# First stage of a hybrid RWKV-7 and neighbourhood-attention layer: another order of loads, modulation pieces and token tiles

## The chip, the cores and the metric

The kernel runs on one core of a Trainium2 chip. The metric is the device time of one execution in microseconds; of several runs the median is taken.

## The reference

One layer of a diffusion backbone works on 512 latent tokens and 128 context tokens of width 1024. Only its beginning matters here:

```python
def _modulation(cvec, w_ada, b_ada):
    m = jax.nn.silu(cvec) @ w_ada + b_ada
    return jnp.split(m[..., None, :], 6, axis=-1)

def _trunk_layer(x, cvec, s0, ctx_k, ctx_v, p):
    sh1, sc1, g1, sh2, sc2, g2 = _modulation(cvec, p["w_ada"], p["b_ada"])
    h = _rmsnorm(x, p["norm1_g"]) * (1.0 + sc1) + sh1
    u_rw, u_na, gate_rw, gate_na = jnp.split(h @ p["w_in"], IN_SPLITS, axis=-1)
    ...
```

A conditioning vector (one for the latent tokens, one for the context tokens) gives a shift and a scale for every channel. The tokens are normalised, scaled and shifted to `h`, and `h` is multiplied by the input weights. Everything else of the layer (the two branches, their merging, the feed-forward part) follows and is the same in both kernels.

## The kernel before

The 640 tokens are five tiles of 128: tiles 0 to 3 are latent, tile 4 is the prompt. The 1024 channels are eight chunks of 128. The first stage has these parts, all in one loop body written out by hand:

- `x_load(i)` loads token tile i (512 KB). `norm_x(i)` normalises it (ScalarE squares, GpSimd takes the power, VectorE scales into `xn`), transposes it on TensorE in eight pieces (`xt`, line 408) and copies it to `xT`, four chunks by VectorE and four by ScalarE.
- `ada_part(k0, n, c0)` is a generator that loads the modulation's weights (`wa`, line 392) for the n chunks from k0 on, and multiplies them with the conditioning vectors on TensorE (`psa`, line 261, a narrow matmul with 32 columns of weights). Each call of `next` issues one load of 512 KB and the matmuls of the load before: one step.
- `mod_part(k0, n, c0)` copies the result out of PSUM (`rows`), transposes it (`pc`, line 419), forms the factors `A` and `B`, and then computes `h` for its chunks: ScalarE the high part (line 432), VectorE the exact value `ht` (line 434) and the low part (line 436). High and low parts let each product be formed from three single matmuls. It does tokens 0 to 511 first, and after a `yield` the prompt.
- `wload` loads a 512 KB piece of projection weights (`wst`, two buffers), casts it to a high part `whi` on ScalarE (line 192) and a low part `wlo` on VectorE (line 195); each has two buffers. A piece serves two chunks.
- `tok_gen` is the projection of one block of 512 output columns: 5 token tiles x 8 chunks x 3 products = 120 matmuls of 128x512 into five accumulators (`acc`, line 311). The first block's generator is `qg`; three such blocks (q, k, v) follow one another, 360 matmuls in all.

The modulation comes in three pieces: chunks 0 and 1, chunks 2 and 3, and chunks 4 to 7. The table `qp` says how many matmuls of `qg` stand between one modulation step and the next:

```python
    qp=((0, 0, 7, 6, 7), (2, 5, 4, 4, 3, 2, 5, 3, 1)), ada=2, pa=1, pd=0,
```

Within this stage TensorE runs in the order in which the code is written. The other engines and the queue of the SyncE engine (SP), which issues almost all loads, get their order from a scheduler at build time. It puts loads that later stages need into the queue where it sees room: the tables of relative positions (`win`, line 858), small projection weights (`upw`, `gup`, line 615 and after), and weights for the second modulation (`f` and `wa`, line 1025).

Of the kernel before, what the change touches and what calls it, by code (L numbers as in the profile page):

```python
# [15 lines left out]
NT = 640  # L16
# [98 lines left out]
def body(ctx: ExitStack, tc: tile.TileContext, xs, xp, cols, consts, w_ada, b_row, w_rw, w_qkv,  # L115
# [88 lines left out]
    def wload(src, eng=None):  # L204
        return wcast(wdma(src), eng)
# [78 lines left out]
            pass  # L284
        return pss

    def tok_gen(pss, pp, lhs_hl, chunks, kts, toks, tag="acc", bufs=5, tail=1, keep=None, eng=None, late=()):


        pss.update((i, pp.tile([P, 512], F32, tag="tp" if i == 5 else tag, bufs=3 if i == 5 else bufs,  # L290
                               name=nm("acc"))) for i in toks)
        lhs = lhs_hl if callable(lhs_hl) else lambda p_, kt, ts_: lhs_hl[p_][:, kt, ts_]
        last = len(kts) - 1
        ws, n0 = [] if keep is None else keep, len(chunks) - tail
        for ci, src in enumerate(chunks):
            ws.append(src if isinstance(src, (tuple, list)) else wload(src, eng))
            ks = [2 * ci + k for k in range(2)]

            if ci >= n0:
                order = [(ki, i) for i in toks for ki in range(2 * n0, last + 1)] if ci == len(chunks) - 1 else ()  # L300
            else:
                order = [(ki, i) for tk in (toks[:4], toks[4:]) for ki in ks for i in tk]
            ns = ((0, 1), (2,)) if ci in late else ((0, 1, 2),)
            for n, ki, i in ((n, *p_) for g in ns for p_ in order for n in g):
                kt = kts[ki]
                hi, lo = ws[ki // 2]
                ts_ = slice(min(i, 4) * 128, min(i, 4) * 128 + 128)
                a, b = (256 * (i - 4), 256 * (i - 3)) if i > 3 and 5 in toks else (0, 512)
                cs_ = slice(ki % 2 * 512 + a, ki % 2 * 512 + b)
                for x, w in (((0, hi), (1, hi), (0, lo))[n],):  # L310
                    pe.matmul(pss[i][:, a:b], lhs(x, kt, ts_), w[:, cs_], start=ki == 0 and n == 0,  # L311
                              stop=ki == last and n == 2)
                    yield
# [42 lines left out]
    hh, hl = hilo("h")  # L356
# [23 lines left out]
    xt, q0 = [], []  # L380

    def x_load(i):
        x = sb.tile([P, 1024], F32, tag="x", bufs=XB, name=nm("x"))
        sp.dma_start(x, xs[i * 128:(i + 1) * 128, :] if i < 4 else xp)
        xt.append(x)

    def wa_load(k0, n, kt):

        w = sb.tile([P, 1024], F32, tag="wa", bufs=WAB, name=nm("wa"))
        for i in range(4 // n):  # L390
            wv = w_ada[(kt + i) * 128:(kt + i + 1) * 128, 0:2048].rearrange("p (g c) -> p g c", g=2)
            sp.dma_start(V(w[:, :], [[128 * n, 2], [1, 128 * n]], i * 256 * n), wv[:, :, 128 * k0:128 * (k0 + n)])
        return w

    def ada_part(k0, n, c0):
# [7 lines left out]
    def norm_x(i):  # L403
        xn = tok_norm(sb, xt[i])
        for q in range(2):
            ps = pp.tile([P, 512], F32, tag="tp", name=nm("xt"))
            for k in range(4):
                pe.transpose(ps[:, k * 128:(k + 1) * 128], xn[:, (4 * q + k) * 128:(4 * q + k + 1) * 128], ident)
            (act.copy if q else dve.tensor_copy)(xT[:, 4 * q:4 * q + 4, i * 128:(i + 1) * 128],
                                                 V(ps[:, :], [[128, 4], [1, 128]]))  # L410

    def mod_part(k0, n, c0):

        m_ = n // 2
        rows = sb.tile([P, 256], F32, tag="rows", bufs=1, name=nm("rows"))
        dve.tensor_copy(rows[:, :64 * n], psa[:, c0:c0 + 64 * n])
        pc = pp.tile([P, 512], F32, tag="tp", name=nm("pc"))
        for q in range(m_):
            pe.transpose(pc[:, q * 128:(q + 1) * 128], rows[:, q * 128:(q + 1) * 128], ident)
        for j, m in ((2, A), (3, A), (0, B), (1, B)):  # L420
            kt = k0 + m_ * (j % 2)
            dve.tensor_tensor(out=m[:, kt:kt + m_, :], in0=V(pc[:, :], [[128, m_], [1, 2]], 32 * j),
                              in1=V(C[:, :], [[1, m_], [0, 2]], CO["bada"] + 8 * (j // 2) + kt), op=ALU.add)
        ks = slice(k0, k0 + n)
        dve.scalar_tensor_tensor(out=A[:, ks, :], in0=A[:, ks, :], scalar=1.0,
                                 in1=V(C[:, :], [[1, n], [0, 2]], CO["n1"] + k0), op0=ALU.add, op1=ALU.mult)
        for g, (a, b) in enumerate(((0, 512), (512, NT))):
            if g:
                yield
            for kt in range(k0, k0 + n):  # L430
                t = sb.tile([P, 512], F32, tag="ht", bufs=2, name=nm("ht"))[:, :b - a]
                act.activation(hh[:, kt, a:b], xT[:, kt, a:b], AF.Identity, bias=B[:, kt, g:g + 1],
                               scale=A[:, kt, g:g + 1])
                dve.tensor_scalar(out=t, in0=xT[:, kt, a:b], scalar1=A[:, kt, g:g + 1],
                                  scalar2=B[:, kt, g:g + 1], op0=ALU.mult, op1=ALU.add)
                dve.tensor_tensor(out=hl[:, kt, a:b], in0=t, in1=hh[:, kt, a:b].bitcast(F32), op=ALU.subtract)  # L436
# [5 lines left out]
    with s0:  # L442
        with tc.manual_schedule(engines=START):
            g = ada_part(0, 2, 0)
            for i in range(4):
                x_load(i)
                next(g, None)
                if i:
                    norm_x(i - 1)
            for _ in g:  # L450
                pass
            norm_x(3)
            q0.append(wload(w_qkv[0]))
            x_load(4)
            mod = mod_part(0, 2, 0)
            next(mod)
            psq = {}
            qg = tok_gen(psq, pp, (hh, hl), q0 + [w_qkv[i] for i in range(1, 4)], list(range(8)), range(5))
# [7 lines left out]
            g = ada_part(2, 2, 128)  # L466
            for i, n in enumerate(PRM["qp"][0]):
                next(g, None)
                some_q(n)
                if i == 2:  # L470
                    norm_x(4)
                    drain(mod)
            drain(mod_part(2, 2, 128))
            g = ada_part(4, 4, 256)
            for n in PRM["qp"][1]:
                next(g, None)
                some_q(n)
            drain(mod_part(4, 4, 256))
# [133 lines left out]

    def prep_dma(ct, S, upw, eng=sp):
        S.upw = upw
        eng.dma_start(upw[:, 0:512], lup[ct, :, 0:512])
        S.gup = kp.tile([P, 128], F32, tag="gup", bufs=2, name=nm("gup"))
        eng.dma_start(S.gup, lup[ct, :, 512:640])

    def prep_cast(S):
        upw = S.upw  # L620
# [219 lines left out]
    with s1:  # L840
# [13 lines left out]
        def window(ft, n):  # L854

            hd, ty = divmod(n, 3)
            win = p1.tile([P, 249], F32, tag="win", bufs=2, name=nm("win"))
            sp.dma_start(win[:, :249], bass.AP(rpbp.tensor, rpbp.offset + (2 * ft + hd) * 465 + 8 * ty,
                                               [[1, 16], [31, 8], [1, 249]]))
            bm = bms[(ft % 2) * 6 + n]  # L860
            pool.tensor_tensor(
                out=V(bm[0][:, :], [[bm[2], 2], [8, 16], [1, 8]], bm[1]),
                in0=V(win[:, :], [[-16, 2], [-1, 16], [-31, 8]], 248),
                in1=V(nam[:, :], [[16, 2], [1, 16], [0, 8]], 32 * ty), op=ALU.add)
# [69 lines left out]
        with ExitStack() as s1b:  # L934
# [86 lines left out]
            def ada_w(g, kt):  # L1021
                ws = [tb.tile([P, 1024], F32, tag="wa", bufs=2, name=nm("wa")), f5()[:, 0:1024]]
                for i, w in enumerate(ws):
                    c = g * 2048 + i * 1024
                    sp.dma_start(w, w_ada[kt * 128:(kt + 1) * 128, c:c + 1024])
                return ws

            def ada_gen():
# [1151 lines left out]
```

## Time and profile before

| | |
|---|---|
| three runs | 1141.27, 1141.41, 1143.85 us; median 1141.41 us |
| profiled execution, from its first to its last instruction | 1142.3 us |
| TensorE busy with matmuls | 97% of the span |
| VectorE, ScalarE, GpSimd busy | 68%, 47%, 17% |
| first stage, up to the first matmul of the second projection block | 62.6 us |

The profile is one execution of its own. It lists no time beside its span, which lies between the shortest and the longest of the runs. In its rows PE is the matmul part of TensorE and PEld its loading of weights, DVE is VectorE, ACT is ScalarE, POOL is GpSimd and SP is the queue of loads. L311 is line 311 of the kernel. A row of the time line has a start, a length in us, the engine, and what was done; in square brackets stands how long the engine was idle before, and what ended that. PEclk is the clock that TensorE was granted, 1.00 being full speed. A busy matmul's length includes its way through the array, so that matmuls overlap in the rows; their pace is read from their starts.

### The profile page before, as it was taken

To read this page: it belongs to the slowest core of one execution; us is meant where nothing else is said; L and a number is where in the kernel's file an instruction comes from. 1 tells how busy PE (TensorE), PEld (TensorE's weight loads), DVE (VectorE), ACT (ScalarE), POOL (GpSimd) and SP (SyncE) were. 2 spreads that over 40 slices of the span, in tenths; PEclk is the share of its full clock that TensorE was granted. 3 is DMA by queue.
4 is the path that set the end of the run, shared out by engine and by line. 5 is a ranking of instruction groups with operands and counts; after the bars stand their busy time and mean duration, and the time that the engine had idled before them with its cause. 6 is when DMAs were issued, how large, how long until landed. Compare 5 with 4: busy or idle time off the path is not lost.

```text
span 1142.3 us, 26868 instructions
## 1 busy us (share of the span) xinstructions
PE 1108.0 (97%) x11160; PEld 980.2 (86%) x11160; DVE 777.2 (68%) x1641; ACT 537.9 (47%) x1060; POOL 195.8 (17%) x262
## 2 busy tenths in 40 slices
PE   5999999999999999999899999999999999999998
PEld 4688878789888988888898788999899989998997
DVE  4565465669658847945787846996478647874775
ACT  4444566665565665567343525654134413441340
POOL 1163244330101212110100511210101010101000
PEclk8999999999999999999999999999999999999999
DMA  9753677654423433344734962223212321232122
GB/s 340 262 107 102 187 268 259 200 151 112 126 64 98 130 104 94 107 108 107 266 92 126 264 214 72 78 89 112 72 56 93 111 74 56 93 106 80 56 93 93
DMA packets 60482, 149.16 MB, mean 131 GB/s; under 512 B 7460, under 2 KB 22436, under 8 KB 60360
## 3 DMA queue, kind: packets, MB, share of 16 engines
q1 hardware_dynamic: 54312, 129.85, 34.8%
q0 software_dynamic: 4032, 14.68, 6.5%
q10 hardware_dynamic: 2016, 2.90, 0.8%
q8 instruction: 88, 1.44, 0.5%
q14 instruction: 34, 0.28, 0.1%
HBM read 118.41 MB, written 14.32 MB: 116 GB/s over the span
## 4 chain that ended last, share of the span: by engine, by line
PE 76%; DVE 8%; issue 7%; ACT 4%; DMA 3%; POOL 1%; SPq 0%; ACTq 0%; DVEq 0%; POOLq 0%
PE acc L311 23%; PE f L1883 23%; PE fl L223 10%; PE mm L223 5%; DMA wa<-in_w_ada_dram 3%; PE psa L1044 1%; DVE RL L1330 1%; DVE pr L1326 1%; PE lg L959 1%; PE pt L988 1%; PE po L1006 1%; DMA win<-in_rpbp_dram 1%; PE w L1446 1%; PE fl L587 1%; PE w L1189 1%
## 5 line engine op out<-in xcount | busy, mean ns | idle before, releaser
L1883 PE MATMUL f<-t,whi 128*128 128x320 f32 x640 | 141.7, 310 | 0.2
L311 PE MATMUL acc<-whi,u 128*128 128x512 f32 (+1 forms) x448 | 136.1, 386 | 0.0
L1883 PE MATMUL f<-b,whi 128*128 128x320 f32 x608 | 135.0, 310 | 0.4 <-DVE b L212 0.4
L223 PE MATMUL fl<-h,whi 128*128 128x320 f32 x672 | 120.9, 320 | 0.0
L1883 PEld LDWEIGHTS f<-t,whi 128*128 128x128 f32 x640 | 106.8, 188 | 0.8 <-issue 0.4
L223 PEld LDWEIGHTS fl<-h,whi 128*128 128x128 f32 x672 | 101.2, 188 | 4.8 <-issue 0.2
L192 ACT CAST whi<-wst 128x1024 fp32r<-128x1024 f32 (+1 forms) x77 | 79.3, 1033 | 53.4 <-PE acc L311 41.6
L1883 PEld LDWEIGHTS f<-b,whi 128*128 128x128 f32 x608 | 101.8, 188 | 1.1 <-issue 0.6
L1883 PE MATMUL f<-t,wlo 128*128 128x320 f32 x320 | 98.9, 309 | 0.0
L311 PEld LDWEIGHTS acc<-whi,u 128*128 128x128 f32 x448 | 83.5, 188 | 16.6
L1883 PE MATMUL f<-b,wlo 128*128 128x320 f32 x304 | 94.1, 309 | 0.0
L1936 ACT CAST whi<-ws 128x1024 fp32r<-128x1024 f32 x40 | 42.0, 1051 | 104.4 <-PE f L1883 45.6
L1950 POOL TENSOR_TENSOR ws<-wst 128x512 f32<-128x512 f32 x20 | 29.2, 1462 | 334.6 <-DVE wlo L1939 226.3
L311 PE MATMUL acc<-wlo,u 128*128 128x512 f32 (+1 forms) x224 | 86.3, 385 | 0.0
L311 PE MATMUL acc<-whi,h 128*128 128x512 f32 x240 | 79.2, 404 | 0.8 <-DVE h L436 0.8
L195 DVE TENSOR_TENSOR wlo<-wst,whi 128x1024 fp32r<-128x1024 f32 (+2 forms) x57 | 60.2, 1066 | 27.8 <-ACT whi L192 27.2
L1751 DVE SCALAR_TENSOR_TENSOR tt<-acc,G 128x512 f32<-128x512 f32 (+1 forms) x51 | 34.7, 680 | 59.6 <-PE acc L311 44.7
L223 PE MATMUL fl<-h,wlo 128*128 128x320 f32 x336 | 62.7, 318 | 0.0
L1936 ACT CAST whi<-wst 128x1024 fp32r<-128x1024 f32 (+1 forms) x48 | 41.3, 869 | 42.3 <-PE acc L311 37.6
L1883 PEld LDWEIGHTS f<-t,wlo 128*128 128x128 f32 x320 | 60.1, 188 | 0.0
L1939 DVE TENSOR_TENSOR wlo<-ws,whi 128x1024 fp32r<-128x1024 f32 x40 | 55.5, 1387 | 5.4 <-ACT whi L1936 5.4
L191 POOL DMA_DIRECT2D wlo<-wst x28 | 24.8, 886 | 191.4 <-ACT wlo L190 169.9
(341 smaller groups left out, 2534.0 us busy)
## 6 DMA issues: line engine op xcount, KB each, us to landing
wst<-in_w_dram SPq DMA_DIRECT2D x66, 512.0 KB
wst<-in_w_rw_dram SPq DMA_DIRECT2D x31, 512.0 KB
wlo<-wst POOLq DMA_DIRECT2D x28, 512.0 KB, 4.7
wa<-in_w_ada_dram SPq DMA_DIRECT2D x24, 512.0 KB
f<-in_w_ada_dram SPq DMA_DIRECT2D x16, 512.0 KB
wst<-in_w_qkv_dram SPq DMA_DIRECT2D x12, 512.0 KB
o<-o_d SPq DMA_DIRECT2D x14, 320.0 KB
x<-in_xs_dram SPq DMA_DIRECT2D x8, 512.0 KB
```

The lines of the kernel that those rows point to most:

```text
L191: pool.dma_start(lo[:, :n].bitcast(F32), st[:, :n], accum_op=ALU.add)
L192: act.copy(hi[:, :n], st[:, :n])
L195: dve.tensor_tensor(out=lo[:, a:b], in0=st[:, a:b], in1=hi[:, a:b].bitcast(F32), op=ALU.subtract)
L223: pe.matmul(ps[:, :t1 - t0], w[:, a:a + 128], x[:, k0 + kt, t0:t1], start=n == 0, stop=n == 3 * nk - 1)
L311: pe.matmul(pss[i][:, a:b], lhs(x, kt, ts_), w[:, cs_], start=ki == 0 and n == 0, stop=ki == last and n == 2)
L587: pe.matmul(ps[hf][:, :H2], u[:, kt * 128:kt * 128 + 128], x[:, kt, a:b], start=kt == 0 and n == 0, stop=kt == 7 and n == 2)
L959: pe.matmul(psl[:, hd, o_:o_ + n], qT[ft][rows, qs], x[rows, :], start=True, stop=True)
L1751: dve.scalar_tensor_tensor(out=tt, in0=ps[:, a:b], scalar=c, in1=G[:, g, sl], op0=ALU.mult, op1=ALU.mult)
L1883: pe.matmul(ps[:, :H2], w_[:, c_], x_[:, kt, :], start=first and kt + n == 0, stop=last and kt == 3 and n == 2, skip_group_check=more)
L1936: act.copy(r[0][:, :width], src())
L1939: dve.tensor_tensor(out=r[1][:, :width], in0=src(), in1=r[0][:, :width].bitcast(F32), op=ALU.subtract)
L1950: eng_x(PRM["se"][i - 1]).tensor_tensor(out=o_, in0=x, in1=y, op=op)
```

## The change

Four edits go together in the first stage.

1. Loads of later stages (`win`, the second modulation's weights, and the first `upw` and `gup`) are pinned behind the last modulation weights that the code has issued for this stage, by an ordering without a wait on an engine (`pin`).
2. The modulation comes in four pieces of two chunks each. The loads for chunks 4 to 7 are sixteen transfers of 256 KB where eight of 512 KB were. The first piece computes `h` in three groups of tokens: 0 to 255, 256 to 511, and the prompt.
3. The prompt's tile is loaded later, and its matmuls on the first two pieces of projection weights come behind those of the other four tiles (`steps`).
4. `qp` is now three rows of small commands: a number is so many matmuls, `a` a modulation step, `w` the load of the second piece of projection weights, `x` and `n` load and normalise the prompt's tile, `m` finishes a piece of modulation and modulates the latent tokens, `t` modulates the prompt's for the pieces done so far.

```diff
-    qp=((0, 0, 7, 6, 7), (2, 5, 4, 4, 3, 2, 5, 3, 1)), ada=2, pa=1, pd=0,
+    qp=("a a w 7 a x 3 a 2 m 12", "a 6 a 6 n a t 6 a 3 m 9", "t 6 a a 6 a 6 a 3 m t"), ada=2, pa=1, pd=0,
...
-            ws.append(src if isinstance(src, (tuple, list)) else wload(src, eng))
+            ws.append(src if isinstance(src, (tuple, list)) else src() if callable(src) else wload(src, eng))
...
+            if steps and ci < len(steps):
+                order = steps[ci]
...
+    urgent = []
+
+    def pin(ins):
+        tc.add_manual_dep(ins.ins, urgent[-1].ins.name, mybir.DependencyInfo(
+            mybir.DependencyClass.NoSync, mybir.DependencyReason.DATA), reason="order")
...
-    def mod_part(k0, n, c0):
+    def mod_part(k0, n, c0, groups):
...
-        for g, (a, b) in enumerate(((0, 512), (512, NT))):
-            if g:
-                yield
+        for (a, b) in groups:
+            yield
+            g = int(a >= 512)
...
-            norm_x(3)
             q0.append(wload(w_qkv[0]))
-            x_load(4)
-            mod = mod_part(0, 2, 0)
+            g = ada_part(2, 2, 128)
+            next(g)
+            mod = mod_part(0, 2, 0, ((0, 256), (256, 512), (512, NT)))
+            next(mod)
+            norm_x(3)
+            next(mod)
             next(mod)
...
+            steps = ([(k, i) for k in (0, 1) for i in four],
+                     [(2, i) for i in four] + [(0, 4), (1, 4)] + [(3, i) for i in four] + [(2, 4), (3, 4)])
+            chunks = q0 + [lambda: wcast(q0[1])] + [w_qkv[i] for i in (2, 3)]
...
+                    elif e == "m":
+                        drain(g)
+                        mod = mod_part(k0, 2, 64 * k0, ((0, 512), (512, NT)))
+                        next(mod)
+                        next(mod)
+                        todo.append(mod)
+                        if k0 < 6:
+                            g = ada_part(k0 + 2, 2, 64 * k0 + 128)
```

How the instructions stand now is shown at three places. The first is the SP queue behind the first piece's modulation weights (`wst` projection weights, `x` from `in_xp_dram` the prompt's tile). Before:

```order
L174 DMA wst_251<-in_w_qkv_dram 128x1024
L384 DMA x_257<-in_xp_dram 128x1024
L392 DMA wa_284<-in_w_ada_dram 128x2x256 x2
L392 DMA wa_295<-in_w_ada_dram 128x2x256 x2
L392 DMA wa_306<-in_w_ada_dram 128x2x256 x2
L392 DMA wa_356<-in_w_ada_dram 128x2x256 x2
L392 DMA wa_405<-in_w_ada_dram 128x2x512
```

and from there, some rows on:

```order
L858 DMA win_1024<-in_rpbp_dram 128x1x249
L858 DMA win_1027<-in_rpbp_dram 128x1x249
L392 DMA wa_440<-in_w_ada_dram 128x2x512
L615 DMA upw_1217<-in_lup_dram 128x512
L1025 DMA f_221_1297<-in_w_ada_dram 128x1024
L1025 DMA f_260_1486<-in_w_ada_dram 128x1024
L174 DMA wst_543<-in_w_qkv_dram 128x1024
L392 DMA wa_450<-in_w_ada_dram 128x2x512
```

Now:

```order
L174 DMA wst_232<-in_w_qkv_dram 128x1024
L400 DMA wa_238<-in_w_ada_dram 128x2x256 x2
L400 DMA wa_301<-in_w_ada_dram 128x2x256 x2
L400 DMA wa_312<-in_w_ada_dram 128x2x256 x2
L174 DMA wst_315<-in_w_qkv_dram 128x1024
L400 DMA wa_337<-in_w_ada_dram 128x2x256 x2
L386 DMA x_340<-in_xp_dram 128x1024
L400 DMA wa_384<-in_w_ada_dram 128x2x256 x2
```

```order
L400 DMA wa_579<-in_w_ada_dram 128x2x256 x2
L174 DMA wst_635<-in_w_qkv_dram 128x1024
L887 DMA win_1080<-in_rpbp_dram 128x1x249
L887 DMA win_1083<-in_rpbp_dram 128x1x249
L644 DMA upw_1273<-in_lup_dram 128x512
```

The prompt's tile moved behind four `wa` rows of two transfers each and a piece of projection weights, and `win`, `upw` and `f` behind the last `wa`.

The second place is TensorE at the start of the projection (`h_89` and `h_93` are the high and low parts of chunks 0 and 1). Before:

```order
L408 MATMUL xt_239<-K,xn_233 128x128 x4
L408 MATMUL xt_245<-K,xn_233 128x128 x4
L419 MATMUL pc_261<-K,rows_259 128x128
L261 MATMUL psa<-wa_284,cs 32x128 x8
L261 MATMUL psa<-wa_295,cs 32x128 x8
L311 MATMUL acc_309<-whi_253,h_89 128x512
L311 MATMUL acc_309<-whi_253,h_93 128x512
```

Now:

```order
L428 MATMUL pc_243<-K,rows_241 128x128
L417 MATMUL xt_257<-K,xn_251 128x128 x4
L417 MATMUL xt_263<-K,xn_251 128x128 x4
L261 MATMUL psa<-wa_238,cs 32x128 x8
L261 MATMUL psa<-wa_301,cs 32x128 x8
L313 MATMUL acc_317<-whi_234,h_89 128x512
L313 MATMUL acc_317<-whi_234,h_93 128x512
```

`pc` moved ahead of the transposes of token tile 3.

The third place is the prompt's tile and the third modulation piece, which stands only in the change: on TensorE

```order
L417 MATMUL xt_421<-K,xn_415 128x128 x4
L417 MATMUL xt_427<-K,xn_415 128x128 x4
L261 MATMUL psa<-wa_405,cs 32x128 x8
L313 MATMUL acc_321<-whi_234,h_89 128x512
L313 MATMUL acc_321<-whi_234,h_93 128x512
```

and, six matmuls and a step later,

```order
L313 MATMUL acc_317<-wlo_388,h_90 128x512
L261 MATMUL psa<-wa_474,cs 32x128 x8
L428 MATMUL pc_490<-K,rows_488 128x128
L313 MATMUL acc_318<-whi_387,h_90 128x512
L313 MATMUL acc_318<-whi_387,h_94 128x512
```

and on VectorE

```order
L445 TENSOR_TENSOR h_94<-ht_456,h_90 128x128
L195 TENSOR_TENSOR wlo_545<-wst_542,whi_544 128x1024
L425 COPY rows_488<-psa 128x128
L431 TENSOR_TENSOR A<-pc_490,C 128x2 x2
L431 TENSOR_TENSOR B<-pc_490,C 128x2 x2
```

The accumulator of the prompt's tile (`acc_321`) starts right behind one modulation step, `pc_490` follows its last step with no matmul between, and the `rows` that it reads stands behind a `wlo` on VectorE.

More of the change, by code (lines that the diff above doesn't have):

```diff
@@ L285, in tok_block, with tok_gen @@
         return pss
-    def tok_gen(pss, pp, lhs_hl, chunks, kts, toks, tag="acc", bufs=5, tail=1, keep=None, eng=None, late=()):
+    def tok_gen(pss, pp, lhs_hl, chunks, kts, toks, tag="acc", bufs=5, tail=1, keep=None, eng=None, late=(), steps=None):
         pss.update((i, pp.tile([P, 512], F32, tag="tp" if i == 5 else tag, bufs=3 if i == 5 else bufs,
@@ L391, in wa_load @@
             wv = w_ada[(kt + i) * 128:(kt + i + 1) * 128, 0:2048].rearrange("p (g c) -> p g c", g=2)
[L392 removed]
+            urgent.append(sp.dma_start(V(w[:, :], [[128 * n, 2], [1, 128 * n]], i * 256 * n),
+                                       wv[:, :, 128 * k0:128 * (k0 + n)]))
         return w
@@ L451, in body @@
                 pass
+            q0.append(wload(w_qkv[0]))
+            g = ada_part(2, 2, 128)
+            next(g)
+            mod = mod_part(0, 2, 0, ((0, 256), (256, 512), (512, NT)))
+            next(mod)
             norm_x(3)
-            q0.append(wload(w_qkv[0]))
-            x_load(4)
-            mod = mod_part(0, 2, 0)
+            next(mod)
             next(mod)
             psq = {}
-            qg = tok_gen(psq, pp, (hh, hl), q0 + [w_qkv[i] for i in range(1, 4)], list(range(8)), range(5))
+            four = list(range(4))
+            steps = ([(k, i) for k in (0, 1) for i in four],
+                     [(2, i) for i in four] + [(0, 4), (1, 4)] + [(3, i) for i in four] + [(2, 4), (3, 4)])
+            chunks = q0 + [lambda: wcast(q0[1])] + [w_qkv[i] for i in (2, 3)]
+            qg = tok_gen(psq, pp, (hh, hl), chunks, list(range(8)), range(5), steps=steps)
             derived()
@@ L464, in some_q @@
                     next(qg)
[L466 to L478, printed above, removed]
+            todo = [mod]
+            for k0, row in zip((2, 4, 6), PRM["qp"]):
+                for e in row.split():
+                    if e.isdigit():
+                        some_q(int(e))
+                    elif e == "a":
+                        next(g, None)
+                    elif e == "w":
+                        q0.append(wdma(w_qkv[1]))
+                    elif e == "x":
+                        x_load(4)
+                    elif e == "n":
+                        norm_x(4)
+                    elif e == "t":
+                        while todo:
+                            drain(todo.pop(0))
+                    elif e == "m":
[6 more added lines that the diff above has]
+                            g = ada_part(k0 + 2, 2, 64 * k0 + 128)
             tc.keep_in_program_order(act.dma_start(K[:, 128:], consts[:, 128:KO["nam"]]))
@@ L614, in prep_dma @@
         S.upw = upw
-        eng.dma_start(upw[:, 0:512], lup[ct, :, 0:512])
         S.gup = kp.tile([P, 128], F32, tag="gup", bufs=2, name=nm("gup"))
-        eng.dma_start(S.gup, lup[ct, :, 512:640])
+        for dst, a, b in ((upw[:, 0:512], 0, 512), (S.gup, 512, 640)):
+            ins = eng.dma_start(dst, lup[ct, :, a:b])
+            if not ct:
+                pin(ins)
     def prep_cast(S):
@@ L857, in window @@
             win = p1.tile([P, 249], F32, tag="win", bufs=2, name=nm("win"))
-            sp.dma_start(win[:, :249], bass.AP(rpbp.tensor, rpbp.offset + (2 * ft + hd) * 465 + 8 * ty,
-                                               [[1, 16], [31, 8], [1, 249]]))
+            pin(sp.dma_start(win[:, :249], bass.AP(rpbp.tensor, rpbp.offset + (2 * ft + hd) * 465 + 8 * ty,
+                                                   [[1, 16], [31, 8], [1, 249]])))
             bm = bms[(ft % 2) * 6 + n]
```

2 lines of the change are left out of this document (1 added, 1 removed).

## The prediction

> **What bounds the kernel now.** I read the page's busy shares and slices first, then the chain of waits over the first 130 us, then busy times by stretch, and last the time line of TensorE and VectorE from 14 to 63 us.
>
> ```profile
> PE 1108.0 (97%) x11160; PEld 980.2 (86%) x11160; DVE 777.2 (68%) x1641; ACT 537.9 (47%) x1060; POOL 195.8 (17%) x262
> ...
> PEclk8999999999999999999999999999999999999999
> ```
>
> TensorE is the bound of the whole. Only the first slices leave it free, so a first stage that ends earlier moves everything behind it by as much.
>
> ```profile
> 14.60 7.02 DMA wa<-in_w_ada_dram
> 21.64 9.98 DMA win<-in_rpbp_dram
> ...
> 31.69 9.39 DMA wa<-in_w_ada_dram
> ...
> 46.16 8.22 PE acc L311 x36
> ```
>
> The chain names loads up to 41 us, one of them a `win` that nobody needs yet: 9.98 us. That invites the reading "some 10 us to win". The busy times say otherwise.
>
> ```profile
> core 0: us, PE busy (x) PEld busy (x) DVE busy (x) ACT busy (x) POOL busy (x), PEclk, DMA share, GB/s
> ...
> 14.83:18.25 3.42, 2.02 (x28) 1.30 (x26) 2.09 (x5) 1.91 (x4) 0.54 (x1) 1.00 1.04 388
> 18.25:21.66 3.41, 2.29 (x34) 0.96 (x34) 3.34 (x11) 3.15 (x5) 0.84 (x1) 1.00 1.11 350
> 21.66:25.07 3.41, 2.65 (x7) 2.07 (x7) 1.41 (x3) 0.00 (x0) 0.00 (x0) 0.50 1.06 372
> 25.07:28.49 3.42, 3.42 (x26) 2.50 (x25) 1.59 (x4) 1.30 (x3) 0.00 (x0) 0.50 1.05 390
> ...
> 31.90:40.00 8.10, 8.01 (x57) 3.92 (x59) 5.52 (x15) 3.65 (x6) 0.00 (x0) 1.00 1.04 403
> 40.00:62.60 22.60, 22.42 (x120) 16.31 (x113) 12.86 (x31) 11.82 (x19) 6.95 (x14) 1.00 0.61 181
> ```
>
> From 25 us on TensorE is hardly ever idle, although the DMA engines are full until 42 us. Two other things cost time: TensorE starts its real work only at 22 us, and from 21.66 to 28.49 it runs at clock 0.50.
>
> ```profile
> 18.58 0.33 PE L419 MATMUL pc<-K,rows 128*128 128x128 f32 x1 [0.35 <-DVE xT L409]
> ...
> 20.91 0.43 PE L261 MATMUL psa<-wa,cs 128*32 128x128 f32 x8 [0.32 <-DMA wa<-in_w_ada_dram]
> 21.27 0.49 PE L311 MATMUL acc<-whi,h 128*128 128x512 f32 x1
> 22.52 0.80 PE L311 MATMUL acc<-whi,h 128*128 128x512 f32 x1 [0.76 <-DVE h L436]
> ...
> 25.24 1.91 PE L408 MATMUL xt<-K,xn 128*128 128x128 f32 x8
> ...
> 29.52 0.40 PE L311 MATMUL acc<-whi,h 128*128 128x512 f32 x1
> 29.85 0.65 PE L261 MATMUL psa<-wa,cs 128*32 128x128 f32 x16
> 30.42 0.50 PE L311 MATMUL acc<-whi,h 128*128 128x512 f32 x1
> 30.76 0.39 PE L311 MATMUL acc<-wlo,h 128*128 128x512 f32 x1
> ...
> 59.01 0.39 PE L311 MATMUL acc<-wlo,h 128*128 128x512 f32 x1
> ...
> 62.64 0.62 PE L311 MATMUL acc<-whi,h 128*128 128x512 f32 x2
> ```
>
> ```profile
> L311 PE MATMUL acc<-whi,h x80: 387/394/796, 21.3 to 62.2; 128*128 128x512 f32 x80
> L311 PE MATMUL acc<-wlo,h x40: 387/390/632, 23.1 to 62.4; 128*128 128x512 f32 x40
> ```
>
> The first projection block is 120 matmuls, and the next block begins at 62.64: that is the milestone I forecast. The pace is (62.64 - 59.01) / 16 = 0.227 us a matmul. A modulation step (`psa`) adds (30.76 - 29.52) - 2 x 0.227 = 0.79 us. Check of this reading: from 22.52, 119 matmuls (27.0), 10 steps (7.9), eight transposes of token tile 4 (1.1, estimated as the 1.91 above at full clock, with its gaps), the last `pc` and the transposes of the context keys (1.2 estimated) make 37.2; 62.64 - 22.52 is 40.1. The missing 2.9 is nearly the clock's loss, worked out below. So waits for loads behind 22.52 cost almost nothing in this execution.
>
> **The change part by part.** The edits meet at the same milestone, so each is priced there.
>
> *Loads.* Ahead of the last modulation weights five loads go away (two `win`, `upw`, two `f`; 0.12 x 2 + 0.25 + 0.5 x 2 MB, some 4 us of full DMA engines at 370 GB/s). Eight 512 KB transfers become sixteen of 256 KB. In 18.25 to 21.66 only such small pieces moved, at 350 GB/s: 0.75 us a piece. From 16.5 us, when the first projection weights have landed (row below), 24 pieces and three 512 KB loads (1.3 us each at about 400 GB/s) end at 16.5 + 18 + 3.9 = 38.4. By the sum below TensorE wants that piece only at about 48, so earlier landing is worth little: what the rows make late is TensorE itself.
>
> ```profile
> PEld psa L261 <- DMA wa<-in_w_ada_dram: 1.0, 2, 0.5
> ...
> PEld pc L419 <- DVE rows L416: 0.4, 1, 0.4
> ```
>
> Behind 28.5 us these are the only load waits for modulation weights worth naming: 1.0 us, of which about 0.7 is the gap that every step has. Gain 0.3. Against it, the fourth load of the second piece lands at about 23.8, just when TensorE asks for it: -0.3 to 0. I take 0 for both together.
>
> [...]
>
> The moved loads have cover: `f` is read at 140 us, `win` at 53.6 us, and both would land by about 44 (38.4 plus 4, plus their issue).
>
> ```profile
> 140.31 1.85 PE psa L1044 x16
> ```
> ```profile
> 53.62 1.79 POOL L861 TENSOR_TENSOR bm<-win,nam 128x256 f32<-128x256 f32 x2
> ```
>
> *Earlier start.* The prompt's tile is loaded later, so the second piece's weights land 1.3 us earlier (512 KB), and the first matmul can go at 20.0 instead of 21.27. The second one waits for VectorE:
>
> ```profile
> 16.94 0.28 DVE L416 COPY rows<-psa 128x128 f32<-128x128 f32 x1
> ...
> 18.44 1.21 DVE L195 TENSOR_TENSOR wlo<-wst,whi 128x1024 fp32r<-128x1024 f32 x1
> 19.57 0.22 DVE L422 TENSOR_TENSOR A<-pc,C 128x2 f32<-128x2 f32 x2
> ...
> 20.03 1.01 DVE L434 TENSOR_SCALAR ht<-xT,A,B 128x512 f32<-128x512 f32 x2
> ...
> 21.78 1.29 DVE L436 TENSOR_TENSOR h<-ht,h 128x512 fp32r<-128x512 f32 x2
> ```
>
> `pc` now goes ahead of the transposes: `rows` ends at 17.2, `pc` at 17.6, the factors take 0.4 as above (18.1), the copy of `xT` 0.7 (18.8), two half-width `ht` 0.6 (19.4, estimated a little over half of 1.01), `wlo` 1.2 (20.6), the first half-width `h` 0.35 (20.9). So 22.52 becomes 20.9: gain 1.6. Bounds: 2.5 (start at 20.0 without a wait) and 0.
>
> *The clock.* In the low stretch line 311 did this:
>
> ```profile
> 22.52:28.49 5.97, 3.33 (x7) 2.23 (x8) 0.50 1.05 385
> ```
>
> Seven matmuls, eight transposes and a step would take 1.6 + 1.1 + 0.8 = 3.5 us at full clock: the low clock costs 5.97 - 3.5 = 2.5 us. It set in after 18.25 to 21.66, which held one of these matmuls and otherwise narrow `psa` ones (128*32). The stretch before it, with eleven transposes and `psa`, kept clock 1.00. Under the change the critical stretch gets four matmuls of 512 columns (one at 20.0, three from 20.9) and the end of tile 3's transposes. That is nearer to the stretch that kept its clock: I take a full clock, gain 2.5. Bounds: 2.5 and -0.5 (the same low stretch, with more work inside it).
>
> *Token tile 4 last.* Its transposes are followed by one step and then at once by its own matmuls. Now the chain behind the transposes runs:
>
> ```profile
> 27.67 0.88 ACT L432 ACTIVATE h<-xT,B,A 128x128 fp32r<-128x128 f32 x2
> ```
> ```profile
> 28.20 0.68 DVE L436 TENSOR_TENSOR h<-ht,h 128x128 fp32r<-128x128 f32 x2 [0.53 <-ACT h L432]
> ```
>
> From the transposes' end (25.24 + 1.91 = 27.15) `h` is there 1.0 us later and its low part at 28.6. The step covers 0.8. Cost 0.4 (bounds 0 and 0.8).
>
> *Four pieces.* A fourth `pc` round. Two of them now follow their last step directly: `rows` (0.28) and `pc` with nothing in between, about 0.6 each; one round had 0.7 before with its 0.4 of waiting above. The third piece is worse: VectorE has `wlo` of chunk 2 ahead of its `rows`. That needs `whi`, whose buffer comes free only when tile 4's matmuls on chunk 0 end.
>
> ```profile
> 16.57 1.05 ACT L192 CAST whi<-wst 128x1024 fp32r<-128x1024 f32 x1 [0.76 <-DMA wst<-in_w_qkv_dram]
> ```
>
> Chain: 1.05 + 1.21 + 0.28, with hand-overs 2.75 us. TensorE has step, three matmuls, step in between, 2.2 us: 0.5 more. Together 0.6 + 0.6 + 0.5 - 0.7 = 1.0 us of loss (bounds 0 and 2).
>
> **Sum:** 62.64 - 1.6 - 2.5 + 0.4 + 1.0 = 59.9, a gain of 2.7 us. Nothing behind the milestone absorbs it, since TensorE is dense there. The profiled execution spans 1142.3 us, 0.9 above the median of 1141.41 and inside the runs (1141.27 to 1143.85). Against the median: 1138.7 us. A measurement here can tell about 0.3%, or 3.4 us.
>
> **Rivals.** *The clock falls as before.* For it: `psa` still fills 18.8 to 20.0, and VectorE still holds the second matmul. The gain is then 1.6 - 0.5 - 1.4 = -0.3: 1141.7. With one low stretch instead of two, 1.3 of the 2.5 is kept: 1139.9.
>
> [...]
>
> *The waits do not appear.* The start comes at the bound of 2.5, and tile 4 and `pc` cost half: 2.5 + 2.5 - 0.7 = 4.3 gained, 1137.1. For it: the schedule leaves VectorE idle for much of 22 to 26 us. Against it: the order of VectorE above.
>
> *Slower: small pieces run below 180 GB/s.* Tile 4's load stands behind eight pieces, and its transposes hold TensorE in order. At 0.75 us a piece it lands at 16.5 + 2.6 + 6.0 = 25.1, is normalised 3.5 us later (28.6), and is wanted at 31.6. The 3.0 of slack and the 2.7 gained are gone at 0.75 + 5.7 / 8 = 1.46 us a piece (180 GB/s); at 1.9 us the kernel takes 1144.9. Against it: 350 GB/s.
>
> **How the numbers follow.** Forecast 0.40 (1138.7). Clock low twice 0.23 (1141.7), once 0.15 (1139.9). No waits 0.14 (1137.1). Small pieces 0.08 (1144.9). Faster by over 0.3% takes 3.4 us: the fourth, and about a third of the forecast's own spread of half a microsecond to a full one: 0.28. Slower by 0.3%: the last, and little of the second: 0.09. Same: 0.63. The range leaves out about 2 in 10: 1136.9 to 1141.8.
>
> **What would show it.** The first projection matmul at 20.0 and the second near 20.9; no clock of 0.50 behind 18 us; a `win` load after the last modulation weights, landed near 38; an idle gap of about a microsecond ahead of the third `pc`; the second block's first matmul near 59.9. I am wrong if the clock still falls, if `psa` waits for loads behind 24 us, or if the gain up to the milestone is lost behind it.

## The result and the profile after

| | before | changed |
|---|---|---|
| runs, us | 1141.14, 1141.27, 1141.41, 1143.85; median 1141.34 | 1154.75, 1155.33, 1156.03, 1160.79; median 1155.68 |
| profiled execution, first to last instruction | 1142.3 us | 1153.0 us |
| first matmul of the second projection block | 62.64 us | 60.26 us |

The ratio is 1.0123, 95% interval 1.0104 to 1.0142: slower by about 14 us, where 2.7 us of gain were forecast. Yet the first stage does what was forecast. Its rows of TensorE's time line, in the profile of the changed kernel (start, length, work, and in brackets the idle time before it and what ended that):

```profile
19.83 0.50 PE L313 MATMUL acc<-whi,h 128*128 128x512 f32 x1
21.04 0.50 PE L313 MATMUL acc<-whi,h 128*128 128x512 f32 x1 [0.72 <-DVE h L445]
...
34.54 0.82 PE L313 MATMUL acc<-whi,h 128*128 128x512 f32 x2 [0.49 <-ACT h L441]
...
38.74 0.33 PE L428 MATMUL pc<-K,rows 128*128 128x128 f32 x1 [0.41 <-DVE rows L425]
...
49.33 0.33 PE L428 MATMUL pc<-K,rows 128*128 128x128 f32 x1 [0.41 <-DVE rows L425]
...
60.26 0.61 PE L313 MATMUL acc<-whi,h 128*128 128x512 f32 x2
```

The busy times of the changed kernel by stretch, cut as they were for the kernel before (the seventh entry, ahead of the DMA share, is the granted clock):

```profile
core 0: us, PE busy (x) PEld busy (x) DVE busy (x) ACT busy (x) POOL busy (x), PEclk, DMA share, GB/s
...
18.25:21.66 3.41, 2.69 (x40) 1.92 (x41) 3.41 (x8) 2.52 (x5) 0.00 (x0) 1.00 1.07 372
21.66:25.07 3.41, 2.98 (x36) 1.59 (x38) 2.21 (x4) 1.05 (x1) 0.00 (x0) 1.00 1.07 378
25.07:28.49 3.42, 3.42 (x22) 2.61 (x23) 2.01 (x10) 2.12 (x4) 0.54 (x1) 1.00 1.10 348
...
40.00:60.26 20.26, 19.85 (x142) 14.83 (x141) 12.71 (x31) 11.60 (x20) 5.99 (x12) 1.00 0.64 218
```

The clock stays at 1.00 where it was 0.50, and the chain of waits now leaves the loads behind 25 us for TensorE:

```profile
17.14 7.84 DMA wa<-in_w_ada_dram
25.45 0.67 PE acc L313 x2
```

So 2.4 us are won by 60 us. They are still there when the third projection block ends (its last matmul starts at 119.24, before 121.57). From there to the first matmul of the output projection (line 313, at 655.35; line 311, at 644.72 before) the changed kernel takes 536.11 us where the kernel before takes 523.15. I call this the **middle stretch**: it is longer by 13.0 us, although the diff touches nothing in it and the instructions stand in the same order on every engine. Matched matmul for matmul, the lag against the kernel before comes in jumps (times of the kernel before): -2.1 us at 259 us, +2.9 at 282, +4.7 at 377, +9.9 at 443, +11.1 at 540, +10.6 at 655.

The page shows little of it:

```profile
PE 1109.9 (96%) x11224; PEld 984.6 (85%) x11224; DVE 777.6 (67%) x1651; ACT 539.2 (47%) x1062; POOL 194.5 (17%) x262
...
PEclk9999999999999998999999999999999999999999
```

The waits of TensorE show it. Here are its rows of idle time that no semaphore explains ("issue"): total us, times, longest. First the kernel before, then the changed one:

```profile
PE w L1210 <- issue: 3.8, 3, 1.9
PE w L1213 <- issue: 0.9, 1, 0.9
PE w L1189 <- issue: 0.8, 1, 0.8
PE w L1268 <- issue: 0.8, 1, 0.8
```
```profile
PE w L1242 <- issue: 5.1, 3, 2.2
PE w L1239 <- issue: 4.6, 2, 3.5
PE w L1218 <- issue: 4.5, 2, 2.5
PE w L1297 <- issue: 1.0, 1, 1.0
```

By these rows 6.3 us became 15.2. The lines are those of the RWKV branch, where small 64x64 matmuls follow one another. One such burst, on TensorE's time line of the kernel before, and the same burst in the changed kernel:

```profile
278.28 1.16 PE L1268 MATMUL w<-K,f 64*64 64x64 f32 x64
...
281.01 0.30 PE L1213 MATMUL w<-R__2901,f 64*64 64x64 f32 x8
281.24 0.85 PE L223 MATMUL fl<-h,wlo 128*128 128x320 f32 x4
```
```profile
276.60 1.16 PE L1297 MATMUL w<-K,f 64*64 64x64 f32 x64
...
279.04 0.23 PE L1286 MATMUL w<-ZV,J 64*64 64x64 f32 x2
282.76 0.27 PE L1239 MATMUL w<-AG,f 64*64 64x64 f32 x2 [3.50 <-issue]
```

192 matmuls of 64x64 run in 2.8 us before (14.7 ns each). In the changed kernel 165 of them run, then TensorE stands for 3.50 us and waits for nothing that a semaphore tells. Busy times from 260 to 290 us, before and after:

```profile
260.00:290.00 30.00, 29.43 (x627) 28.11 (x621) 29.63 (x126) 12.92 (x26) 2.61 (x10) 1.00 0.45 119
```
```profile
260.00:290.00 30.00, 25.45 (x499) 24.29 (x498) 29.66 (x121) 11.85 (x22) 1.85 (x4) 0.94 0.40 105
```

The clock is lower too (0.94): in the middle stretch it stands at 0.50 for 13.65 us, from 282.93, 446.77 and 549.17 on, each time at such a stop or right behind it; before for 3.41 us. At half speed that costs at most 5.1 us more, an estimate: half of 13.65 less 3.41. With 8.9 us more of stops the two account for at most 14.0 us; the stretch measured 13.0.

### The profile page after: what moved, and what is told of

Read it like the earlier page. It is cut to its first block, busy times and chain, and to the rows that moved or that the text cites. A ratio compares the mean times of both kernels' runs of the same rounds, so it can differ in the third digit from the quotient of the medians.

```text
span 1153.0 us, 27020 instructions
## 1 busy us (share of the span) xinstructions
PE 1109.9 (96%) x11224; PEld 984.6 (85%) x11224; DVE 777.6 (67%) x1651; ACT 539.2 (47%) x1062; POOL 194.5 (17%) x262
## 4 chain that ended last, share of the span: by engine, by line
PE 77%; issue 8%; DVE 6%; ACT 5%; DMA 4%; POOL 1%; SPq 0%; ACTq 0%; DVEq 0%; POOLq 0%
PE acc L313 23%; PE f L1912 23%; PE fl L223 12%; PE mm L223 4%; DMA wa<-in_w_ada_dram 2%; PE psa L1073 1%; PE po L1035 1%; PE lg L988 1%; PE pt L1017 1%; PE fl L614 1%; DMA o_d<-on 1%; PE w L1242 1%; PE w L1475 1%; DVE RL L1359 1%; PE w L1218 1%
```

## The experiments

**Theory A.** The trace of the changed kernel shows 88 packets of 16,384 B on a queue of the kind "instruction" (q8), one about every 13 us of its 1153.0 us. The theory takes them for TensorE's instructions, and a stop for the time in which the next packet is not there yet. In the changed kernel the packet behind the stop above begins at 280.32 us and the first matmul after it starts at 282.76, 2.44 us later; the stops that end at 447.34 and 548.74 stand 2.24 and 2.21 us behind packets that begin at 445.10 and 546.53. The change makes 64 more matmul records and 64 more weight loads in the first stage (32 more modulation matmuls, two records each; x11224 for x11160). The kernel before has 88 such packets too, for 22,320 records: 254 to a packet. If each record is one instruction and a packet holds 256 (an estimate from these counts, tested below), the 128 more are half a packet, and every later border between two packets falls at another place in the bursts. **Rivals:** the pinned loads collide with something (B), the new order of the first stage does (C), the windows of low clock fall otherwise because the stage ends earlier (D), or more instructions cost time as such (E).

**The borders alone.** In the kernel before, and nothing else moved on any engine:

```diff
         with tc.manual_schedule(engines=START):
+            for _ in range(32):
+                pe.matmul(psa[0:16, 0:16], mhalf, mhalf, start=True, stop=True)
             g = ada_part(0, 2, 0)
```

> The kernel before, with 32 tiny matmuls (16x16, into PSUM columns that are overwritten later) at the very start, where TensorE still waits for its first load; nothing else is moved on any engine. In the trace each of them should be two matmul records with a weight load each, so TensorE's later instructions stand 128 instructions further on, as they do in the changed kernel. Theory A (TensorE's instructions arrive in blocks of 16 KB, and the place of a block's border inside the bursts of short matmuls decides how long TensorE runs dry): about 1153 to 1157 us, with the low-clock windows of the changed kernel near 283, 450 and 550 us. Rival B (the loads that were pinned behind the modulation's weights collide with something later), rival C (the new order of the first stage) and rival E (more instructions as such, 128 of 22,500): 1141 to 1142 us. Rival D (the clock's windows fall otherwise because the stage ends 2.4 us earlier): 1141 to 1142 us, since here it ends as before.

Measured: 1155.41 us, ratio 1.0109 (1.0086 to 1.0133). TensorE's stops without a semaphore are as long in sum as the changed kernel's, 15.2 us:

```profile
PE w L1191 <- issue: 4.8, 2, 2.6
PE w L1215 <- issue: 4.7, 3, 2.2
PE w L1212 <- issue: 4.1, 2, 3.2
PE w L1270 <- issue: 1.6, 1, 1.6
```

Its middle stretch takes 535.83 us. The whole loss appears in the kernel before, without the change, so none of B, C and D is needed for it. The windows of low clock are others than I expected (264.9 and 452.6, 6.8 us in all), so they follow the stops less closely than A said, and some 2 us of this stretch's loss stay unassigned.

**Twice as many.** The same with `range(64)`, a whole packet:

> The kernel before with 64 tiny matmuls at the start, twice as many as in the first run: 256 instructions, one whole block. Theory A: 1141 to 1143 us, as before, although the program is longer. Rival E, if the first run is slow for its mere length: twice that loss, about 1167 us.

Measured: 1142.86 us, ratio 1.0006 (0.9993 to 1.0018), middle stretch 523.74 us. The longer program costs nothing that can be measured, so E is out: 128 more instructions cost 13 us, 256 more cost none of it.

**The changed kernel with the borders put back.** The same edit with `range(32)` in the changed kernel:

> The changed kernel with the same 32 tiny matmuls at its start: TensorE's later instructions now stand 256 instructions (one block of 16 KB) behind those of the kernel before, so the borders fall where they fell before. Theory A: 1138 to 1140 us, the 2.4 us of the first stage at last in the total. Rivals B, C and D: 1155 to 1156 us. Rival E: 1156 us or more.

Measured: 1141.82 us, ratio 0.9991 (0.9979 to 1.0003); 14 us less than without the tiny matmuls, which run from 1.2 to 2.9 us, while TensorE waits for its first load, though above the 1138 to 1140 that I expected. The pinned loads, the new order and the earlier end of the first stage are all in this kernel and the loss is not: B, C and D are out as its cause. Whether the 2.4 us of the first stage are in the total, this measurement cannot tell, so the kernel was measured again:

> The changed kernel with 32 tiny matmuls at the start once more, in more rounds, since the first measurement (ratio 0.9991, from 0.9979 to 1.0003) cannot tell 2.4 us of gain from none. If the first stage's gain is kept: 0.9979 (2.4 us of 1142). If half of it is lost behind: 0.9990.

Measured: 1140.98 us, ratio 0.9983 (0.9973 to 0.9993): faster, by 1.9 us (0.8 to 3.1). That fits the first stage's gain and does not exclude half of it.

**No pinning.**

```diff
     def pin(ins):
+        return
```

> The changed kernel without the pinning: the loads of later stages stand in the queue where the scheduler puts them, five of them (two win, upw, two f) ahead of the last modulation weights, as before. TensorE's and VectorE's orders are those of the changed kernel. Rival B: 1139 to 1143 us. Theory A, C, D, E: 1154 to 1157 us (first stage perhaps 0 to 1 us later).

Measured: 1159.76 us, ratio 1.0162 (1.0131 to 1.0194), middle stretch 533.04 us: it is long without the pinning too, which speaks against B once more. The pinning itself helps the first stage: without it the last modulation weights land at 43.6 us instead of 39.1, and the second projection block starts at 61.55 instead of 60.26. TensorE's waits from 14 to 62 us name the place (the same row has 2.3 us in the changed kernel):

```profile
PE pc L429 <- DVE rows L426: 4.3, 3, 2.4
```

The total is not the price of the pinning alone. The scheduler also moved a load of output-projection weights ahead of four small loads, at about 650 us, and at 681 us TensorE waits for the low parts of such weights:

```profile
PE acc L313 <- DMA wlo<-wst: 5.1, 1, 5.1
```

The clock stands at 0.50 for 6.83 us from 684.28 on. With both, the lag against the changed kernel goes from -1.8 us at 655 us to +5.2 at 690. That the moved load causes this wait was not tried.

**One part undone.** Chunks 4 to 7 as one piece again takes the 128 instructions out without any tiny matmul:

```diff
-    qp=(..., "a 6 a 6 n a t 6 a 3 m 9", "t 6 a a 6 a 6 a 3 m t"), ...
+    qp=(..., "a 5 a 5 n a t 5 a 5 a 5 a 4 a 4 a 3 m t"), ...
...
-                        mod = mod_part(k0, 2, 64 * k0, ((0, 512), (512, NT)))
+                        mod = mod_part(k0, k0, 64 * k0, ((0, 512), (512, NT)))
...
-                        if k0 < 6:
-                            g = ada_part(k0 + 2, 2, 64 * k0 + 128)
+                        if k0 < 4:
+                            g = ada_part(4, 4, 256)
```

> The changed kernel with one part undone: chunks 4 to 7 are again one piece with eight loads of 512 KB and 32 modulation matmuls where the changed kernel has 64. That takes 128 instructions out of TensorE's stream, the number that the change had added, without any tiny matmul; the other edits stay. Theory A (the place of the 16 KB borders): the borders fall as in the kernel before, so 1139 to 1142 us, with the second projection block at 60 to 62 us. If the loss came from another part of the change (pinning, the late token tile, the three groups of tokens): 1153 to 1157 us.

Measured: 1146.07 us, ratio 1.0031 (1.0016 to 1.0046), outside both expectations. The middle stretch is 522.33 us: all 13 us are gone. But the first stage is worse than I expected. The second block starts at 62.99 (up to 1.7 us of that is a window of low clock, 3.41 us from 47.07), and that block loses 3 us more, 2.4 of them in waits for the norm of the queries and keys:

```profile
PE qt L928 <- ACT q L937: 1.6, 1, 1.6
PE qt L928 <- DVE qn L917: 0.4, 1, 0.4
PE qt L928 <- DVE rs L269: 0.4, 1, 0.4
```

By the end of the third block it is 3.4 us behind the kernel before and 5.7 behind the changed one (its last matmul starts at 124.97, 121.57 and 119.24). So the small pieces of chunks 4 to 7 seem to carry much of the first stage's gain, and they brought the 128 instructions.

**The tiny matmuls in the middle.** In the changed kernel, eight groups of four ahead of the second channel tile's small projections:

```diff
                     x = LX[wi][d]
+                    for _ in range(4 if ct == 1 else 0):
+                        pe.matmul(ps[0:16, 0:16], mhalf, mhalf, start=True, stop=True)
                     pe.matmul(ps[:, :H2], S.uh[:, 2 * wi + d, :], x[:, hf * H2:(hf + 1) * H2],
```

> The changed kernel with the 32 tiny matmuls not at the start but in eight groups of four between 307 and 323 us, ahead of the second channel tile's small projections in the RWKV branch; the order is otherwise unchanged on every engine. Theory A: up to there everything is as in the changed kernel (the lag against the kernel before goes from -2.4 to +2.9 us at 283 us), behind it the borders fall as in the kernel before and the rest of the loss, 7.7 us, does not appear: 1148 us, plus 1 to 3 us for the tiny matmuls in a stretch where TensorE has no idle time, so 1147 to 1151 us. If the loss is set at the beginning (loads, buffers, the order of the first stage): 1156 to 1159 us.

Measured: 1152.61 us, ratio 1.0099 (1.0078 to 1.0119); the profiled execution took 1150.6. The lag (times of the kernel before) goes from -2.4 at 80 us to +2.1 at 281, as in the changed kernel; across the tiny matmuls it rises from 1.1 (300 us) to 4.9 (317), and from there it stays within 0.8 us up to 557 us, where the changed kernel loses another 8 us from 282 to 540. The loss is made locally, burst by burst. The median lies 1.6 us above what I expected at most. The rise of 3.8 us across the tiny matmuls is not theirs alone: a window of low clock, 3.41 us from 308.48 on, is worth up to 1.7 of it, and the rest is within the 1 to 3 expected.

**Other places for the borders.** The changed kernel with `range(16)`, `range(48)`, `range(24)`, `range(36)`:

> The changed kernel with 16 tiny matmuls at the start: borders three quarters of a block behind those of the kernel before (the changed kernel stands at a half). Theory A gives no single number, since it depends on where the bursts of short matmuls lie: the first stage ends near 60.3 us, and what the total has above 1139 us should be found again as idle time of TensorE without a wait, plus windows of low clock. If a border's place does not matter: 1155 us, as the changed kernel.

> The changed kernel with 48 tiny matmuls at the start: borders a quarter of a block behind those of the kernel before. As for 16: Theory A wants the excess over 1139 us to be found as idle time of TensorE without a wait and as windows of low clock; if a border's place does not matter: 1155 us or a little more.

> The changed kernel with 24 tiny matmuls at the start: borders an eighth of a block (32 instructions) away from those of the kernel before. 32 tiny matmuls gave 0.9991 of the kernel before, 16 gave 1.0036. Theory A: between them or near the better one, 1139 to 1147 us, and not 1155.

> The changed kernel with 36 tiny matmuls: borders 16 instructions to the other side of those of the kernel before. 32 gave 0.9991, 48 gave 1.0057. Theory A: 1139 to 1146 us; a shift of 16 instructions of 256 should change few of the stops.

Measured, in the same order: 1146.54, 1149.02, 1145.38 and 1138.85 us. The last is just below what I expected, and its 16 instructions changed more of the stops than I thought.

All runs by the place of the borders, in instructions behind those of the kernel before, modulo 256. "Stops" is the sum of TensorE's idle time without a semaphore, "low clock" the time at 0.50 within the middle stretch, both from the profiled execution:

| kernel | borders | middle stretch, us | stops, us | low clock, us | ratio to before (95%) |
|---|---|---|---|---|---|
| before | 0 | 523.15 | 6.3 | 3.4 | 1 |
| before + 64 | 0 | 523.74 | 4.6 | 10.2 | 1.0006 (0.9993 to 1.0018) |
| before + 32 | 128 | 535.83 | 15.2 | 6.8 | 1.0109 (1.0086 to 1.0133) |
| changed | 128 | 536.11 | 15.2 | 13.7 | 1.0123 (1.0104 to 1.0142) |
| changed, not pinned | 128 | 533.04 | 14.0 | 6.8 | 1.0162 (1.0131 to 1.0194) |
| changed, one piece | 0 | 522.33 | 4.5 | 3.4 | 1.0031 (1.0016 to 1.0046) |
| changed + 32 | 0 | 524.51 | 4.5 | 10.2 | 0.9991 (0.9979 to 1.0003) |
| changed + 32, again | 0 | 522.99 | 5.8 | 3.4 | 0.9983 (0.9973 to 0.9993) |
| changed + 36 | 16 | 520.90 | 2.4 | 3.4 | 0.9964 (0.9950 to 0.9978) |
| changed + 48 | 64 | 527.53 | 7.0 | 6.8 | 1.0057 (1.0039 to 1.0075) |
| changed + 16 | 192 | 526.80 | 8.2 | 3.4 | 1.0036 (1.0023 to 1.0049) |
| changed + 24 | 224 | 525.67 | 9.9 | 3.4 | 1.0016 (1.0005 to 1.0027) |
| changed + 32 in the middle | 128, then 0 | 532.09 | 9.4 | 10.2 | 1.0099 (1.0078 to 1.0119) |

Kernels with borders at the same place agree whatever their first stage (522.3 to 524.5 us at 0, 533.0 to 536.1 at 128), and by and large the stretch grows with the stops. Low clock adds its part: of the two executions of changed + 32 the one with 6.8 us more of it takes 1.5 us longer, although it has 1.3 us less of stops. If all the stops are taken off each stretch, and half of the low clock above 3.4 us, 516 to 519 us are left in every row but the last, which has the tiny matmuls inside the stretch. So these two account for the 15 us between the rows to within some 3 us. The best is 36 tiny matmuls: 1138.85 us against 1143.32 on that chip, faster than both kernels. Its lag of -1.95 us at 80 us is the first stage's, and the middle stretch is 2.25 us shorter than before. Its stops:

```profile
PE w L1244 <- issue: 1.0, 2, 0.7
PE w L1220 <- issue: 0.6, 1, 0.6
PE fl L223 <- issue: 0.4, 1, 0.4
PE w L1401 <- issue: 0.4, 1, 0.4
```

The traces also tell directly where the stops lie. Number TensorE's rows from 0 in the order of their starts, with matmuls, weight loads and the semaphore instructions that the trace lists among them, and divide each number by 256. In all 14 traces of this case, that of the next experiment included, every row that ends a stop (idle time over 0.15 us put down to "issue") leaves the remainder 193 or 194, in 96 stops of 96. It also starts 2.2 to 3.4 us after the packet before it began. So the stops lie a multiple of 256 rows apart, give or take one, and each behind a packet: at the borders, as A has it. Why the remainder is 193 or 194 and not 0 the traces do not show. The changed kernel stops at 8 borders and passes the others.

**The supply by itself.** In the kernel before:

```diff
+            for _ in range(512):
+                pe.matmul(psa[32 * (_ % 4):32 * (_ % 4) + 16, 0:16], mhalf, mhalf, start=True, stop=True)
```

> The kernel before with 512 tiny matmuls at the start, which take turns in the four column groups of TensorE as the modulation's do: 1,024 matmul records and as many weight loads, 2,048 instructions, eight blocks of 16 KB. It is made to read the supply by itself, so only the stretch of the tiny matmuls counts and not the total (20 to 30 us longer). Theory A: they run in bursts of 7 to 15 ns a record, with stops in which TensorE waits for no semaphore; the fetches of blocks stand at least 3.3 us apart, so about 27 us for the whole (8 x 3.4), less what is in store at the start. If the supply is no limit: no stops, fetches as close as 1.8 us (256 instructions at 7 ns for two), 7 to 15 us for the whole.

TensorE's time line of it:

```profile
1.15 2.05 PE L445 MATMUL psa<-mhalf 128*16 128x16 f32 x223 [1.15 <-POOL mhalf L265]
7.42 1.26 PE L445 MATMUL psa<-mhalf 128*16 128x16 f32 x128 [4.21 <-issue]
14.16 1.26 PE L445 MATMUL psa<-mhalf 128*16 128x16 f32 x128 [5.48 <-issue]
...
32.75 1.26 PE L445 MATMUL psa<-mhalf 128*16 128x16 f32 x128 [5.21 <-issue]
36.20 1.26 PE L445 MATMUL psa<-mhalf 128*16 128x16 f32 x128 [2.19 <-issue]
39.66 0.42 PE L445 MATMUL psa<-mhalf 128*16 128x16 f32 x33 [2.19 <-issue]
```

Between the first group, of 223, and the last every group has exactly 128 matmuls, with as many weight loads: 256 records. The queue of instructions moves 8 packets more than in the kernel before (packets, MB, share; first before, then this kernel), for 1,024 matmuls and 1,024 loads:

```profile
q8 instruction: 88, 1.44, 0.5%
```
```profile
q8 instruction: 96, 1.57, 0.5%
```

So 2,048 records more took 8 packets more, 256 to a packet: here a record is one instruction, and the change's 128 are half a packet, as estimated. Most borders of the changed kernel show no stop (8 stops with 88 packets), but in bursts of short matmuls a border cost up to 3.5 us there, and 2.2 to 5.5 us here.

A group starts 2.4 to 2.6 us after its packet begins (7.42 after 5.02, 36.20 after 33.79). Where the DMA engines are idle (share 0.01) the packet begins as the last matmul of the group before starts (33.79 and 33.82), and a group follows every 3.46 us. Where loads fill them (share 1.04), it begins 2.4 to 3.1 us later, and the distance is 5.9 to 6.7 us. Busy times of the two stretches (the last two columns are the DMA engines' share and GB/s):

```profile
8.49:30.18 21.69, 3.96 (x407) 3.57 (x394) 2.13 (x3) 2.19 (x3) 0.55 (x1) 1.00 1.04 356
33.82:39.66 5.84, 1.45 (x152) 1.26 (x139) 0.00 (x0) 0.00 (x0) 0.00 (x0) 1.00 0.01 3
```

My 27 us for the whole were too few (1.15 to 39.9, 38.7 us): I had not thought of the loads. That the packets wait in line behind the loads is an inference from these two stretches; it was not tried apart.

## Why the prediction was wrong

- **Earlier start** (20.0 and 20.9 forecast): 19.83 and 21.04. Right.
- **Clock** (full, 2.5 us): 1.00 throughout the first stage in this execution. Right, and not by the luck of one execution: of the nine other traces with the change or most of it, seven have no low clock before 60 us, and two have one window of 3.41 us (from 18.76 and from 47.07).
- **Token tile 4** (0.4 us of waiting): 0.49. Right.
- **Four `pc` rounds** (1.0): two waits of 0.41, 0.8. Right in size; the wait for the third piece was no longer than that for the fourth.
- **Loads** (0 for all): the `win` loads did land at about 38 to 42 us, but the pinning is not worth 0. Without it the block starts 1.3 us later. With the small pieces under way the DMA engines moved 348 to 378 GB/s, so the rival of slow small pieces is out; behind 24 us the `psa` matmuls wait for loads only 0.24 and 0.19 us (their weight loads 1.9 us, in four waits).
- **The milestone** (59.9): 60.26, a gain of 2.4 for 2.7.
- **"Nothing behind the milestone absorbs it, since TensorE is dense there"**: this is the step that failed. TensorE is dense by the slices and by the 97%, but the waits of the kernel before list 6.3 us in which it stood for no semaphore, all in bursts of short matmuls, and I did not read them: they are a bound of their own, which the runs above put down to the supply of instructions (with 128 more and nothing else moved, 15.2 us). The change's 64 matmul records were priced by their own time in the first stage, and at nothing as instructions. As instructions they cost 13.0 us in the middle stretch, more than five times what the stage gained: 8.9 us of stops and up to 5.1 of low clock.
- **The slower rival** (small pieces below 180 GB/s) did not come, and the last clause of what would prove me wrong, a gain lost behind the milestone, had no mechanism and no price, though it is what came. The range had no room for it.

The forecast of 1138.7 is close to what the change gives with the borders where they were: 0.9983 of 1141.41 is 1139.5 (1138.3 to 1140.6), and by the first measurement, 0.9991, it is 1140.4 (1139.0 to 1141.8). That some of the first stage's gain is lost behind it even then is not excluded.

## What to carry to other kernels

Idle time of TensorE that the waits put down to "issue" within bursts of short matmuls was a bound like any other here (2.4 to 15.2 us in the table above): look for it before forecasting that a gain far ahead of it comes through. Instructions added to TensorE ahead of such bursts moved the borders of all later packets here (128 of them cost 13 us, 256 nothing that can be measured), so count an edit's instructions modulo the packet that the trace shows (other engines were not tried); two versions can be compared fairly when each is also run with its borders shifted by a few places. A few tiny matmuls where TensorE waits anyway are a cheap knob, worth here some 14 us in the changed kernel and, at 36, 0.36% under the kernel before; the next edit may move the borders again.

## What the runs showed of the hardware

- The run of 512 tiny matmuls has 2,048 TensorE records and 8 packets more than the kernel before: 256 to a packet. There TensorE took 128 matmuls with their loads in 1.1 us (8.4 ns each), but with the DMA engines idle (share 0.01) such a group came only every 3.46 us, and beside full ones (1.04) every 5.9 to 6.7 us. In none of the 14 traces do two packets behind the program's start begin less than 3.2 us apart.
- All 96 stops in these traces stand at a packet's border, by the remainder 193 or 194 of 256 and 2.2 to 3.4 us behind a packet's beginning.
- A window of 3.41 us or more at clock 0.50 begins at or right behind 7 of the 15 stops of 2 us or more in the middle stretches. That the stop brings the window is not shown: the run of 512 tiny matmuls has seven stops of 2.2 to 5.5 us at its start and a clock of 1.00 throughout them, and eight traces have a window that begins between 303 and 310 us, with no stop in the 15 us ahead of it.
- What added instructions cost in these bursts depends on where they put the borders: nothing that can be measured for 256, 1.1% for 128, and with 272 the changed kernel is at 0.9964, the first stage's gain included.
